# The last steps of the second FFN product in another order, with five instead of four steps that put off P2 and Q4

## The chip, the cores and the metric

The kernel runs on one core of one Trainium2 chip. What counts is the device time of one execution, in microseconds (us). The kernel before takes 1906.04 us (median of 3 runs, 1905.92 to 1906.49).

## The reference, cut to what matters

One layer of a decoder trunk for 520 tokens (512 of a prompt, 8 single ones), in float32. The change touches only the end of it: the second product of the MLP, the residual and the last norm.

```python
x = x + jnp.einsum('blm,md->bld', mix, p['w_out'][l])
hf = rms_norm(x, p['norm_ffn'][l])
ff = jnp.square(jax.nn.relu(jnp.einsum('bld,df->blf', hf, p['w_ff1'][l])))   # 2048 -> 8192
x = x + jnp.einsum('blf,fd->bld', ff, p['w_ff2'][l])                         # 8192 -> 2048
y = rms_norm(x, p['norm_final'])
```

## The kernel before

Features lie on the 128 partitions and the 520 tokens along a row, in two halves of 260 (`c0` and `c1`). The second FFN product has 64 k-tiles of 128 (the 8192 inner features) and 16 output tiles `X[m]`. k-tiles are taken in 32 pairs and outputs in 8 pairs (`ma`, `mb`), and each 2x2 block product is done with seven products instead of eight: P1, P2, P3, Q4, P5, P6, P7 (table `PROD`). Their left sides are the four weight blocks `w11`, `w12`, `w21`, `w22` and four sums of them, `s1` to `s4`; VectorE makes the sums (`sums`, line 1128). Each left side is split into a high part, by ScalarE (`whi`, line 1172), and a low part, by VectorE (`wlo`, line 1174); TensorE then does three matmuls of 260 columns for each pair of k-tiles (lines 1194, 1196, 1197).

A *step* (`Quad` in the code) is one output pair over a stretch of pairs of k-tiles. `ENDS` and `windows()` list the 44 steps of the second product, numbered 0 to 43 here: for every step the output pair `i` and the pairs of k-tiles. The number of pairs in a step is its width; all its operations are 128 columns wide for each pair, so a step of width 7 has weights of 896 columns, and one of width 2 has 256. The last eight steps before are: 36 to 39, output pairs 4 to 7, width 7 each; 40 to 43, output pairs 0 to 3, widths 5, 4, 3 and 2.

The order of work is written out in `items`: for each step P1, then P3 of the step before it, P2, Q4 of the step before it, P6, P7, P5. Steps 40 to 43 are *late*: their P2 and Q4 are left out there and come at the end of the list, behind everything else. P2 and Q4 add only to the columns `c0`, so that after the last other product the columns `c1` of all outputs are done. The main loop goes through `items`, one per iteration; it issues the sums and the split of the item three ahead (`split_item`), then the matmuls of the item (`product`), and what follows from its result (`ff2_done`), some of it put off by one or more iterations (`after`). Each engine runs its own instructions in the order in which they are issued. `whi` and `wlo` have 4 buffers each; the raw weights have 7 (`NRAW`), loaded on SyncE's queue (`more_weights`, line 1098), which waits until a buffer's last reader is done. P2 and Q4 of a late step load `w12` and `w22` a second time.

The last norm needs the sum of squares over all features. A step that ends its output pair (`q.done`) squares the finished tiles (`sq`; ScalarE, line 982). For a step that is not late, VectorE adds the square of the whole tile to one of two tiles `fsum` (line 977). A late step finishes its tiles in four halves, and each half's square goes to TensorE, which adds it over the partitions with a matmul by ones into the tile `side` (`feature_sum`, line 964); this text calls such a matmul a *sum*. At item `H1_DONE`, the first of the products put off, TensorE also sums the two `fsum` tiles, and from two items later `last_norm(1)` runs between the products: square root on ScalarE, a reciprocal and three operations on VectorE (lines 1243 to 1246), then 16 products with the norm (line 1250) three per item, and their stores. When all products are done, `last_norm(0)` does the same for `c0`.

Of the kernel before, what the change touches and what calls it, by code (L numbers as in the profile page):

```python
# [43 lines left out]
class Gap:  # L44


    def __init__(self, n=2):
# [2 lines left out]

ENDS = ((3, 4, 5, 6, 7, 7, 7, 7), (9, 10, 11, 12, 13, 13, 13, 13), (15, 16, 17, 18, 19, 19, 19, 19),
        (21, 22, 23, 24, 25, 25, 25, 25), (27, 28, 29, 30, 32, 32, 32, 32), (32,) * 8)

# [1 line left out]
PAIRS = (30, 0, 1, 2, 31) + tuple(range(3, 30))  # L59


def windows():

    at = [0] * 8
    for ends in ENDS:
        for i, e in enumerate(ends):
            if e > at[i]:
                yield i, at[i], e
                at[i] = e


def trunk_kernel(tc, xT, vecs, w_in, w_out, w_ff1, w2, ca_st, h0_st, cb_st, gate_w, sgu_wT, sgu_b,
# [4 lines left out]
    with ExitStack() as es:  # L77
# [255 lines left out]
        for kh in (0, 1):  # L333
            for j in range(16):
                m = j // 2 + j % 2 * 8 if kh else j
# [16 lines left out]
        quads = []  # L352
# [476 lines left out]
        ffo = [Ops() for _ in range(32)]  # L829
# [136 lines left out]
        def sq(m, sl):  # L966

            n, x = m % 2, X[m][0]
            if fsum[n] is None:
                fsum[n] = cp.tile([128, T], F32, tag=f"ssum{n}", name=nm("fsum"))  # L970
                after(1, lambda: S.activation(out=fsum[n], in_=x, func=AF.Square), "a")
                return
            z = Zt()

            def add():
                if sl is both:
                    V.tensor_tensor(out=fsum[n], in0=fsum[n], in1=z, op=ALU.add)
                else:
                    feature_sum(int(sl is c1), z, m == 7)

            def f():
                S.activation(out=z[:, sl], in_=x[:, sl], func=AF.Square)
                after(1, add, "v" if sl is both else "p")
            after(1, f, "a")
# [68 lines left out]
        off = 0  # L1053
        last_of = {}
        WIN = list(windows())
        for n, (i, a, b) in enumerate(WIN):
            src = w2[off:off + 4 * 128 * 128 * (b - a)].rearrange("(j p c) -> j p c", j=4, p=128)
            quads.append(Quad(src, b - a, [ffo[k] for k in PAIRS[a:b]], i, n, b == 32, n >= 8 * (len(ENDS) - 1)))
            off += 4 * 128 * 128 * (b - a)
            for k in PAIRS[a:b]:  # L1060
                last_of[k] = quads[-1]
# [41 lines left out]
        for q in quads[32:]:  # L1103
            i, a, b = WIN[q.win]
# [77 lines left out]
        def product(k):  # L1182
# [31 lines left out]
            if q.win is None and p == "P1":  # L1214
                if 2 <= q.idx < 18:
                    sum_x1(q.idx - 2)
                elif q.idx == 20:
                    make_S2()
            if q.late and q.idx == 0 and p == "P1":
                add_eps()  # L1220
            (ff1_done if q.win is None else ff2_done)(q, p)

# [215 lines left out]
```

## Time and profile before

| | us |
|---|---|
| median of 3 runs | 1906.04 |
| profiled execution, its own time | 1908.77 |
| its span | 1907.1 |
| TensorE busy (share of the span) | 1885.5 (99%) |
| VectorE busy | 1559.3 (82%) |
| ScalarE busy | 969.3 (51%) |

The profiled execution is a run of its own, so its time stands beside the median and is not one of the three. A matmul of 260 columns has a record of about 0.28 us, but TensorE starts the next one before it ends; the distance from start to start is what a matmul costs. VectorE's records overlap in the same way by somewhat less than 0.1 us. In the timeline the time in square brackets is how long the engine was idle before the instruction, and for what.

### The profile page before, as it was taken

To read this page: it belongs to the slowest core of one execution; us is meant where nothing else is said; L and a number is where in the kernel's file an instruction comes from. 1 tells how busy PE (TensorE), PEld (TensorE's weight loads), DVE (VectorE), ACT (ScalarE), POOL (GpSimd) and SP (SyncE) were. 2 spreads that over 40 slices of the span, in tenths; PEclk is the share of its full clock that TensorE was granted. 3 is DMA by queue.
4 is the path that set the end of the run, shared out by engine and by line. 5 is a ranking of instruction groups with operands and counts; after the bars stand their busy time and mean duration, and the time that the engine had idled before them with its cause. 6 is when DMAs were issued, how large, how long until landed. Compare 5 with 4: busy or idle time off the path is not lost.

```text
span 1907.1 us, 38101 instructions
## 1 busy us (share of the span) xinstructions
PE 1885.5 (99%) x15588; PEld 1879.3 (99%) x15588; DVE 1559.3 (82%) x2186; ACT 969.3 (51%) x1443; POOL 248.4 (13%) x471
## 2 busy tenths in 40 slices
PE   9999999999999999999999999999999999999996
PEld 9999999999999999999999999999999999999996
DVE  7878777575688889889888888877798888888887
ACT  7345445562235666666665666644444444444453
POOL 0000000000000222122112111500312212112000
PEclk9999999999999999999999999999999999999998
DMA  7323223132343666656656556853756657647334
GB/s 253 106 95 115 73 96 114 59 139 104 126 167 124 217 205 211 217 199 218 209 178 212 196 193 207 288 188 102 277 165 235 231 190 237 207 152 259 119 90 135
DMA packets 110832, 329.36 MB, mean 173 GB/s; under 512 B 16320, under 2 KB 25152, under 8 KB 110656
## 3 DMA queue, kind: packets, MB, share of 16 engines
q1 hardware_dynamic: 73200, 205.35, 32.6%
q0 software_dynamic: 36160, 120.37, 17.8%
q8 instruction: 122, 2.00, 0.4%
q10 hardware_dynamic: 1296, 1.19, 0.2%
q14 instruction: 54, 0.44, 0.1%
HBM read 261.71 MB, written 65.15 MB: 171 GB/s over the span
## 4 chain that ended last, share of the span: by engine, by line
PE 96%; DVE 2%; DMA 1%; issue 0%; ACT 0%; SPq 0%; DVEq 0%
PE psA L1197 12%; PE psA L1194 12%; PE psA L1196 12%; PE ps L192 10%; PE ps L190 10%; PE ps L188 10%; PE psD L1194 6%; PE psD L1196 6%; PE psD L1197 6%; PE psB L1197 3%; PE psB L1196 3%; PE psB L1194 3%; DMA raw<-w 1%; DVE X L1250 1%; DVE wlo L1174 0%
## 5 line engine op out<-in xcount | busy, mean ns | idle before, releaser
L1172 ACT ACTIVATE whi<-raw 128x1024 fp32r<-128x1024 f32 (+5 forms) x532 | 489.2, 922 | 327.6 <-PE psD L1196 149.2
L1174 DVE TENSOR_TENSOR wlo<-raw,whi 128x1024 fp32r<-128x1024 f32 (+5 forms) x532 | 559.8, 1053 | 89.6 <-ACT whi L1172 88.1
L1197 PE MATMUL psA<-o,wlo 128*128 128x260 f32 x2048 | 579.3, 283 | 2.1 <-DVE wlo L1174 2.1
L1194 PE MATMUL psA<-o,whi 128*128 128x260 f32 x2048 | 579.1, 283 | 1.0 <-ACT z L1213 0.5
L1196 PE MATMUL psA<-o,whi 128*128 128x260 f32 x2048 | 578.1, 282 | 0.0
L1197 PEld LDWEIGHTS psA<-o,wlo 128*128 128x128 f32 x2048 | 385.6, 188 | 2.5 <-DVE wlo L1174 2.5
L1194 PEld LDWEIGHTS psA<-o,whi 128*128 128x128 f32 x2048 | 385.7, 188 | 1.7 <-ACT z L1213 0.7
L1196 PEld LDWEIGHTS psA<-o,whi 128*128 128x128 f32 x2048 | 385.6, 188 | 0.1
L1128 DVE TENSOR_TENSOR raw<-raw,raw 128x1024 f32<-128x1024 f32 (+6 forms) x304 | 319.3, 1050 | 28.0 <-DMA raw<-w 27.6
L188 PE MATMUL ps<-Ah,whi 128*128 128x260 f32 x1536 | 311.5, 284 | 1.2 <-ACT Ah L367 1.2
L190 PE MATMUL ps<-Al,whi 128*128 128x260 f32 x1536 | 310.8, 284 | 0.0
L192 PE MATMUL ps<-Ah,wlo 128*128 128x260 f32 x1536 | 310.4, 283 | 0.0
L1194 PE MATMUL psD<-o,whi 128*128 128x260 f32 x1024 | 291.1, 284 | 0.0
L1196 PE MATMUL psD<-o,whi 128*128 128x260 f32 x1024 | 289.8, 283 | 0.0
L1197 PE MATMUL psD<-o,wlo 128*128 128x260 f32 x1024 | 288.8, 282 | 0.0
L188 PEld LDWEIGHTS ps<-Ah,whi 128*128 128x128 f32 x1536 | 238.5, 189 | 2.0 <-ACT Ah L367 1.8
L192 PEld LDWEIGHTS ps<-Ah,wlo 128*128 128x128 f32 x1536 | 238.3, 189 | 0.0
L190 PEld LDWEIGHTS ps<-Al,whi 128*128 128x128 f32 x1536 | 237.5, 190 | 0.6 <-DVE Al L370 0.6
L920 POOL DMA_DIRECT2D fx<-o x210 | 114.0, 543 | 819.6 <-DVE o L805 561.8
L1196 PEld LDWEIGHTS psD<-o,whi 128*128 128x128 f32 x1024 | 193.0, 188 | 0.2
L1194 PEld LDWEIGHTS psD<-o,whi 128*128 128x128 f32 x1024 | 192.7, 188 | 0.2
L1197 PEld LDWEIGHTS psD<-o,wlo 128*128 128x128 f32 x1024 | 192.8, 188 | 0.0
(212 smaller groups left out, 2291.5 us busy)
## 6 DMA issues: line engine op xcount, KB each, us to landing
raw<-w_ff SPq DMA_DIRECT2D x128, 512.0 KB, 4.1
fx<-o POOLq DMA_DIRECT2D x210, 260.0 KB, 2.9
o<-fx POOLq DMA_DIRECT2D x210, 260.0 KB, 5.1
raw<-w SPq DMA_DIRECT2D x116, 384.0 KB, 3.8
raw<-w_in SPq DMA_DIRECT2D x62, 512.0 KB, 6.1
raw<-w_out SPq DMA_DIRECT2D x32, 512.0 KB, 5.6
raw<-w SPq DMA_DIRECT2D x32, 448.0 KB, 3.4
z<-x1d POOLq DMA_DIRECT2D x32, 260.0 KB, 3.1
```

The source lines that it names most:

```text
L188: PE.matmul(ps[:, h, :H], hi[:, kk], xh[:, h * H:(h + 1) * H], start=st, stop=False)
L190: PE.matmul(ps[:, h, :H], hi[:, kk], xl[:, h * H:(h + 1) * H], start=False, stop=False)
L192: PE.matmul(ps[:, h, :H], lo[:, kk], xh[:, h * H:(h + 1) * H], start=False, stop=sp)
L920: P.dma_start(fxd[i][2 * g - 1 + n if g else 0], t[0][:, :].bitcast(F32))
L1128: V.tensor_tensor(out=o[0][:, :n], in0=x[0][:, :n], in1=y[0][:, :n], op=ALU.add)
L1172: S.activation(out=whis[i][:, :n], in_=r[0][:, :n], func=AF.Copy)
L1174: V.tensor_tensor(out=wlos[i][:, :n], in0=r[0][:, :n], in1=whis[i][:, :n].bitcast(F32), op=ALU.subtract)
L1194: PE.matmul(ps, hi[:, kk], xh, start=first and j == 0, stop=False, skip_group_check=True)
L1196: PE.matmul(ps, hi[:, kk], xl, start=False, stop=False, skip_group_check=True)
L1197: PE.matmul(ps, lo[:, kk], xh, start=False, stop=j == q.q - 1 and p in (("P2", "P3", "Q4", "P7") if q.late else ("P2", "P3", "Q4")), skip_ ...
L1250: V.scalar_tensor_tensor(out=x, in0=x, scalar=vc(V_FIN + m), in1=o, op0=ALU.mult, op1=ALU.mult)
```

## The change

`ENDS` loses its last row and its steps of width 7 for output pairs 4 to 7; the steps that finish the outputs are now listed by `LAST`, in the order of the output pairs 4, 0, 1, 5, 2, 6, 3, 7. The last eight steps, 36 to 43, thus have the widths 7, 5, 4, 7, 3, 7, 2, 7. The last five of them, 39 to 43 (output pairs 5, 2, 6, 3, 7), are late, where before it was the last four. Steps 0 to 35 are as before. `add_eps` moves with the first late step. The weights in memory (`w2`) follow the order of the steps. Two loads more are issued, since one step more loads `w12` and `w22` twice.

```diff
--- before.py
+++ after.py
@@ -50,8 +50,10 @@
 
 
 
+
+LAST = (4, 0, 1, 5, 2, 6, 3, 7)
 ENDS = ((3, 4, 5, 6, 7, 7, 7, 7), (9, 10, 11, 12, 13, 13, 13, 13), (15, 16, 17, 18, 19, 19, 19, 19),
-        (21, 22, 23, 24, 25, 25, 25, 25), (27, 28, 29, 30, 32, 32, 32, 32), (32,) * 8)
+        (21, 22, 23, 24, 25, 25, 25, 25), (27, 28, 29, 30, 25, 25, 25, 25))
 
 
 
@@ -67,6 +69,8 @@
             if e > at[i]:
                 yield i, at[i], e
                 at[i] = e
+    for i in LAST:
+        yield i, at[i], 32
 
 
 def trunk_kernel(tc, xT, vecs, w_in, w_out, w_ff1, w2, ca_st, h0_st, cb_st, gate_w, sgu_wT, sgu_b,
@@ -976,7 +980,7 @@
                 if sl is both:
                     V.tensor_tensor(out=fsum[n], in0=fsum[n], in1=z, op=ALU.add)
                 else:
-                    feature_sum(int(sl is c1), z, m == 7)
+                    feature_sum(int(sl is c1), z, m == 15)
 
             def f():
                 S.activation(out=z[:, sl], in_=x[:, sl], func=AF.Square)
@@ -1053,9 +1057,10 @@
         off = 0
         last_of = {}
         WIN = list(windows())
+        LATE = len(WIN) - 5
         for n, (i, a, b) in enumerate(WIN):
             src = w2[off:off + 4 * 128 * 128 * (b - a)].rearrange("(j p c) -> j p c", j=4, p=128)
-            quads.append(Quad(src, b - a, [ffo[k] for k in PAIRS[a:b]], i, n, b == 32, n >= 8 * (len(ENDS) - 1)))
+            quads.append(Quad(src, b - a, [ffo[k] for k in PAIRS[a:b]], i, n, b == 32, n >= LATE))
             off += 4 * 128 * 128 * (b - a)
             for k in PAIRS[a:b]:
                 last_of[k] = quads[-1]
@@ -1216,7 +1221,7 @@
                     sum_x1(q.idx - 2)
                 elif q.idx == 20:
                     make_S2()
-            if q.late and q.idx == 0 and p == "P1":
+            if q.win == LATE and p == "P1":
                 add_eps()
             (ff1_done if q.win is None else ff2_done)(q, p)
```

VectorE, from the addition that follows step 41's P3 (the tiles `X`) to the low part of step 43's P6 (step 43 is the last one). Before, where step 42 has width 3 and step 43 width 2:

```order
L998 TENSOR_TENSOR X_15410<-X_15410,psA_23092 128x260
L1128 TENSOR_TENSOR raw_23236<-raw_23130,raw_23196 128x256
L1174 TENSOR_TENSOR wlo_23239<-raw_23130,whi_23238 128x256
L1128 TENSOR_TENSOR raw_23196<-raw_23196,raw_23215 128x256
L1128 TENSOR_TENSOR raw_23130<-raw_23196,raw_23130 128x256
L1174 TENSOR_TENSOR wlo_23258<-raw_23061,whi_23257 128x384
L1032 TENSOR_TENSOR X_15560<-X_15560,psD_23262 128x520
L1128 TENSOR_TENSOR raw_23176<-raw_23130,raw_23176 128x256
L1174 TENSOR_TENSOR wlo_23279<-raw_23130,whi_23278 128x256
```

The same place after the change, where step 42 has width 2 and step 43 width 7:

```order
L1002 TENSOR_TENSOR X_16302<-X_16302,psA_22911 128x260
L1133 TENSOR_TENSOR raw_23090<-raw_22952,raw_23044 128x896
L1179 TENSOR_TENSOR wlo_23093<-raw_22952,whi_23092 128x896
L1133 TENSOR_TENSOR raw_23044<-raw_23044,raw_23060 128x896
L1133 TENSOR_TENSOR raw_22952<-raw_23044,raw_22952 128x896
L1179 TENSOR_TENSOR wlo_23109<-raw_22886,whi_23108 128x256
L1036 TENSOR_TENSOR X_15730<-X_15730,psD_23113 128x520
L1133 TENSOR_TENSOR raw_23015<-raw_22952,raw_23015 128x896
L1179 TENSOR_TENSOR wlo_23127<-raw_22952,whi_23126 128x896
```

The kinds of rows and their order are the same: an addition, the sum `s3` and the low part of step 43's P1, the sums `s1` and `s2`, the low part of step 42's P3, an addition to `X` over both halves, the sum `s4` and the low part of step 43's P6. Those of step 43 are 896 instead of 256 columns wide, and that of step 42 is 256 instead of 384.

VectorE in the part where the products put off run and `last_norm(1)` goes on between them (the low parts are those of the P2 and Q4 put off, `RF` is the norm of the columns c1). Before:

```order
L1174 TENSOR_TENSOR wlo_23469<-raw_23357,whi_23468 128x256
L1002 TENSOR_TENSOR X_15411<-X_15411,psD_23474 128x260
L1250 SCALAR_TENSOR_TENSOR X_15307<-X_15307,vec,RF 128x260
L1250 SCALAR_TENSOR_TENSOR X_15308<-X_15308,vec,RF 128x260
L1250 SCALAR_TENSOR_TENSOR X_15410<-X_15410,vec,RF 128x260
L1174 TENSOR_TENSOR wlo_23496<-raw_23370,whi_23495 128x256
L998 TENSOR_TENSOR X_15559<-X_15559,psB_23501 128x260
L1250 SCALAR_TENSOR_TENSOR X_15411<-X_15411,vec,RF 128x260
L1250 SCALAR_TENSOR_TENSOR X_15559<-X_15559,vec,RF 128x260
L1250 SCALAR_TENSOR_TENSOR X_15560<-X_15560,vec,RF 128x260
L1002 TENSOR_TENSOR X_15560<-X_15560,psD_23521 128x260
```

After the change, at the same point behind the three operations that end in `RF`:

```order
L1179 TENSOR_TENSOR wlo_23423<-raw_23272,whi_23422 128x256
L1002 TENSOR_TENSOR X_16302<-X_16302,psB_23428 128x260
L1255 SCALAR_TENSOR_TENSOR X_15411<-X_15411,vec,RF 128x260
L1255 SCALAR_TENSOR_TENSOR X_15559<-X_15559,vec,RF 128x260
L1255 SCALAR_TENSOR_TENSOR X_15560<-X_15560,vec,RF 128x260
L1179 TENSOR_TENSOR wlo_23459<-raw_23303,whi_23458 128x896
L1006 TENSOR_TENSOR X_16303<-X_16303,psD_23464 128x260
L1255 SCALAR_TENSOR_TENSOR X_15729<-X_15729,vec,RF 128x260
L1255 SCALAR_TENSOR_TENSOR X_15730<-X_15730,vec,RF 128x260
L1255 SCALAR_TENSOR_TENSOR X_15906<-X_15906,vec,RF 128x260
L1179 TENSOR_TENSOR wlo_23495<-raw_23340,whi_23494 128x896
L1002 TENSOR_TENSOR X_15729<-X_15729,psB_23500 128x260
```

Before, the last two low parts (of step 43's P2 and Q4) are 256 wide and are the first and the sixth row behind `RF`; after them come additions and products with the norm alone. Now the low parts of step 43's P2 and Q4 are 896 wide and stand further on, between the products with the norm, each ahead of an addition to `X` that a square and a sum on TensorE follow.

## Rows read from the trace of the kernel before

**Rows 1.** The page, part 1: busy time, share of span, instructions.
```profile
PE 1885.5 (99%) x15588; PEld 1879.3 (99%) x15588; DVE 1559.3 (82%) x2186; ACT 969.3 (51%) x1443; POOL 248.4 (13%) x471
```

**Rows 2.** Busy time by stretch: us, PE, PEld, DVE, ACT, POOL, granted clock, DMA, GB/s.
```profile
1780.00:1842.00 62.00, 62.00 (x520) 62.00 (x519) 51.48 (x66) 29.38 (x40) 0.00 (x0) 1.00 0.32 93
1249.60:1253.20 3.60, 2.97 (x13) 2.67 (x13) 1.63 (x3) 0.00 (x0) 0.00 (x0) 0.54 0.36 118
1884.00:1891.70 7.70, 6.11 (x38) 5.05 (x36) 7.60 (x21) 1.98 (x5) 0.00 (x0) 1.00 0.38 131
```

**Rows 3.** Waits of TensorE: who for whom, total us, times, longest.
```profile
PE side L964 <- ACT z L982: 2.2, 2, 1.4
```

**Rows 4.** Timeline 1881 to 1883: start us, us, engine, line, operation [idle before].
```profile
1881.82 0.28 PE L1197 MATMUL psB<-o,wlo 128*128 128x260 f32 x1
...
1881.93 0.60 PE L964 MATMUL side<-z,ones 128*128 128x260 f32 x2
...
1882.14 0.43 DVE L998 TENSOR_TENSOR X<-X,psB 128x260 f32<-128x260 f32 x1 [0.83 <-PE psB L1197]
...
1882.48 1.77 DVE L1243 RECIPROCAL RF<-z 128x260 f32<-128x260 f32 x1
1882.49 0.28 PE L1196 MATMUL psD<-o,whi 128*128 128x260 f32 x1
```

**Rows 5.** Timeline 1885 to 1888, the same columns.
```profile
1885.20 0.28 PE L1197 MATMUL psB<-o,wlo 128*128 128x260 f32 x1
...
1885.56 0.42 DVE L1174 TENSOR_TENSOR wlo<-raw,whi 128x256 fp32r<-128x256 f32 x1
1885.89 0.42 DVE L1002 TENSOR_TENSOR X<-X,psD 128x260 f32<-128x260 f32 x1
...
1886.41 0.42 ACT L982 ACTIVATE z<-X 128x260 f32<-128x260 f32 x1 [2.10 <-DVE X L1002]
...
1886.88 0.71 PE L964 MATMUL side<-z,ones 128*128 128x260 f32 x2 [1.40 <-ACT z L982]
...
1887.54 0.28 PE L1196 MATMUL psD<-o,whi 128*128 128x260 f32 x1
...
1887.77 0.42 DVE L998 TENSOR_TENSOR X<-X,psB 128x260 f32<-128x260 f32 x1
...
1888.10 1.28 DVE L1250 SCALAR_TENSOR_TENSOR X<-X,vec,RF 128x260 f32<-128x260 f32 x3
...
1889.30 0.42 DVE L1002 TENSOR_TENSOR X<-X,psD 128x260 f32<-128x260 f32 x1
```

**Rows 6.** Timeline, the end of the last product.
```profile
1891.37 0.28 PE L1197 MATMUL psD<-o,wlo 128*128 128x260 f32 x1
...
1892.37 0.42 DVE L1002 TENSOR_TENSOR X<-X,psD 128x260 f32<-128x260 f32 x1
```

**Rows 7.** Timeline of TensorE around step 43's P5 and P3.
```profile
1872.26 0.28 PE L1197 MATMUL psA<-o,wlo 128*128 128x260 f32 x1
1873.02 0.39 PE L1194 MATMUL psA<-o,whi 128*128 128x260 f32 x1 [0.48 <-ACT z L1213]
```

**Rows 8.** Timeline of VectorE and, last, ScalarE: wide operations.
```profile
1823.54 1.08 DVE L1128 TENSOR_TENSOR raw<-raw,raw 128x896 f32<-128x896 f32 x1
1824.54 1.09 DVE L1174 TENSOR_TENSOR wlo<-raw,whi 128x896 fp32r<-128x896 f32 x1
1825.54 0.42 DVE L998 TENSOR_TENSOR X<-X,psA 128x260 f32<-128x260 f32 x1
...
1837.50 0.95 ACT L1172 ACTIVATE whi<-raw 128x896 fp32r<-128x896 f32 x1 [1.23 <-issue]
```

**Rows 9.** DMA issues by line, 1780 to 1880: KB each, median us to landing.
```profile
raw<-w SPq DMA_DIRECT2D x8, 448.0 KB, 3.3
```

**Rows 10.** Tile view of raw, 1780 to 1890: its loads.
```profile
DMA to landing us min/median/max: 2.0/2.9/4.2
```

**Rows 11.** Timeline of TensorE behind its longest pause in the second product.
```profile
1249.59 0.58 PE L1197 MATMUL psA<-o,wlo 128*128 128x260 f32 x1 [1.91 <-DVE wlo L1174]
```

## What the change does to the time, predicted

> **What bounds the kernel now.** I read the page's busy shares first: TensorE is busy for 99% of the span, VectorE for 82%, ScalarE for 51% [rows 1]. A busy share says little of TensorE, because its records overlap, so the next view is the table of stretches: 520 matmuls in the 62 us before the narrow steps, one every 0.119 us, at full granted clock [rows 2]. In wide steps nothing stands between two matmuls. Then come TensorE's waits and the timeline of the last 50 us. There TensorE pauses in two places. Between the last P5 and P3, which share a PSUM tile, it waits for ScalarE's copy: 0.76 us from start to start instead of 0.12 [rows 7]. Among the products put off it waits for squares [rows 3]. That chain is worth following back: the sum at 1886.88 waited for a square at 1886.41, that for an addition on VectorE at 1885.89, and the addition stood in VectorE's order behind the reciprocal of 1882.48, three operations and a low part [rows 4, 5]. So at the end VectorE sets the pace, and TensorE everywhere else. When the last matmul is issued, at 1891.37, its addition starts 1.00 us later, since VectorE is still at the norm of c1; in a case without a queue, 1881.82 to 1882.14, it is 0.32 [rows 4, 6]. What follows that addition is a chain of fixed work for c0 which the change leaves alone.
>
> **What the change does not touch.** Steps 0 to 36 give the same instructions in the same order. The last eight steps have 42 pairs of k-tiles in both orders, so 42 x 7 x 3 = 882 matmuls in both, at 0.119 us each the same 105 us. (A product of width w takes 3 w x 0.119: 2.5 us at 7, 1.07 at 3, 0.72 at 2.) What can differ is what stands between the matmuls.
>
> **Added: four sums on TensorE.** One step more is late, and each late step has four sums of squares by TensorE: 20 instead of 16. (Two full-width `fsum` additions leave VectorE for it, in a place where nobody waits.) A sum costs TensorE 0.67 - 2 x 0.12 = 0.43 us between 1881.82 and 1882.49 [rows 4], and 0.66 - 0.12 = 0.54 us between 1886.88 and 1887.54 [rows 5]. I take 0.5: +2.0 us. All four lie in TensorE's path: two in step 40, where step 39's halves are summed, two behind the first products put off.
>
> **Removed: the pauses at the end before.** From 1885.20 to 1886.88 TensorE loses 1.68 - 0.12 = 1.56 us. From there to 1891.49 (0.12 after the last start) there are 21 matmuls and three sums, 21 x 0.119 + 3 x 0.54 = 4.1 of 4.6 us: 0.5 more [rows 5, 6]. Together -2.06. The last addition no longer queues: 1.00 - 0.32 = -0.68.
>
> **What takes the place of these pauses.** The closing chain keeps its place, two products behind `H1_DONE`, and the products around it are now 40's (width 3), 41's (7), 42's (2) and 43's (7). I count from the moment at which TensorE has issued step 40's P2. VectorE: addition at 0.2, reciprocal at 0.54, low part 3.08 later (1882.48 to 1885.56), the addition for 40's Q4 at 3.95. From an addition's start to its sum is 0.99 us (1885.89 to 1886.88) [rows 4, 5]. That sum can run at 4.94. TensorE arrives there after sum, Q4, sum and 41's P2, 0.5 + 1.07 + 0.5 + 2.5 = 4.57: a pause of 0.4. Then VectorE has three products with the norm (1.20, 1888.10 to 1889.30), a narrow low part (0.33), an addition (0.33), three products, and then a low part of 896 columns, which takes 1.00 (1824.54 to 1825.54) [rows 5, 8]: 41's Q4 is added at 8.36, summed at 9.35; TensorE arrives at 9.16: 0.2. Three more products with the norm and the second wide low part put the addition for 42's P2 at 10.9 and its sum at 11.9, where TensorE arrives at 10.6: 1.3. Behind that VectorE gets ahead, and the two last wide products run free. Together +1.9: step 42 is too short to cover VectorE's work, and that work has grown by the wide low parts. So of the 2.06 us removed nearly all comes back in another place.
>
> **Bursts ahead of a wide step.** Before, a step is at most as wide as the one before it from step 36 on. Now a wide step follows a narrow one three times. Its two sums `s1`, `s2`, the sums `s3` and `s4` and the low parts of P1 and P6 are due on VectorE while TensorE runs the narrow products. For step 43, counted from the end of 41's P3: VectorE's addition at 0.2, then s3, low part, s1, s2 at 1.00 each, 42's low part 0.33, an addition over 520 columns (0.6, between 0.33 for 260 and 1.00 for 896), s4, and the low part of 43's P6 until 7.6. TensorE: two sums, three narrow products of 0.72, P1 2.5, 42's P3 0.72, and 0.24 to the first matmul that takes a low part: 6.6. One wait inside lies on the way: the second sum's square stands on ScalarE behind a wide high part of 0.95 [rows 8] and is 0.4 late. So 1.0 us is lost. For step 41 the same count gives VectorE 7.7 and TensorE 8.0, since step 40's products are 1.07: nothing. For step 39, behind step 38 of width 4, both come out at about 10, if `w21` lands 3.3 us after its issue [rows 9]: 0.2. Together +1.2. The rows before show no step that widens here, so this term has only bounds: 0 (the counts are off by under 1 us each, and TensorE, already at one matmul every 0.119 us, can gain nothing below it), and 3.9, if each of the three is 0.9 later, by the longest landing of 4.2 instead of 3.3 [rows 10]. I keep 1.2, nearest to the rows.
>
> The Trainium skill (VectorE: DVE Perf Modes, The DRAIN you can't avoid) says that "the next op does not start until the 8-stage pipe empties", though it adds that an operation which is not held starts earlier. The rows show starts 1.00 apart for records of 1.08 and 1.09 [rows 8], so by the trace the pipe is not emptied first. By the page's first sentence the burst of step 43 and the two wide low parts at the end would take about 0.7 us more, and the sum below would be +3.0.
>
> **No change elsewhere.** The wait between the last P5 and P3 stays: the copy does not depend on the width [rows 7]. The loads of the products put off, now 448 KB for the wide ones, are issued at least four wide products (4 x 2.5 = 10 us) ahead of their split, against 3.3 to landing [rows 9].
>
> **Sum.** +2.0 - 2.06 + 1.9 + 1.2 - 0.68 = +2.4 us on the profiled execution: span 1907.1 to 1909.5, its own time 1908.77 to 1911.2. That execution stands 2.7 us above the median of the runs; the same +2.4 on the median is 1908.4.
>
> **Rivals.** A measurement of this kernel can tell about 0.2%, 3.8 us, from no change.
>
> *The pauses do go away.* The products put off last longer (52 pairs instead of 28), and if ScalarE and VectorE get to the squares 1 us sooner than I count, only the four sums remain against what is saved: 2.0 - 2.06 - 0.68 + 0.2 = -0.5, 1905.5. Further down, if bursts and sums fill only time that was lost anyway, it is -2.7, 1903.3. For it: VectorE is idle for stretches in wide steps. Against: its order is fixed, and the wide low parts stand ahead of the additions.
> The Trainium skill (Perfetto Trace Analysis, Optimization Strategy) says that where the most-contended engine changes over time, interleaving those regimes may help; here that would be this rival, since narrow steps are VectorE's and wide ones TensorE's. The trace bears out the two regimes, but also that TensorE lost nothing in the narrow steps before.
>
> *Slower: VectorE late for every wide step.* All three bursts start 0.9 late, because a raw buffer comes free only when the narrow step lets go of it and the load lands at 4.2 instead of 3.3 [rows 9, 10]: +2.7. A pause then reaches the 1.91 after which, at 1249.59, the granted clock had a mean of 0.54 over 3.6 us, most of it at the lower level of 1.2 GHz [rows 11, 2]; around the pause of 1.40 at 1886 it stayed at 1.00 [rows 5, 2]. 3.6 x (1 - 0.54) = 1.7 us of work are lost by that. Then 2.4 + 2.7 + 1.7 = +6.8, 1912.8. It decides from pauses of 1.9 us on. Against: the loads of this stretch are small, and no wait of VectorE for one is seen after 1780.
>
> *The change does nothing visible:* the terms cancel; this is the forecast read with 0.2% as a bound.
>
> **Chances.** The forecast, 1907 to 1909.8: 0.50. The pauses gone, or less lost than I count, 1903 to 1907: 0.30, of which 0.04 is faster by over 0.2%. Slower, from 1909.8 up: 0.20. So faster 0.04, same 0.76, slower 0.20. The range is 1904.6 to 1911.0: it takes in the bursts at nothing and the bursts near their upper bound without the clock.
>
> **What would show it.** Right: 40 instead of 32 matmul records for the sums of squares on `side`; TensorE's waits name `side` after ScalarE's square with about 1.9 us among the products put off, the longest just before 43's P2, and `psA` or the low part of step 43's P6 with about 0.6. The last addition starts 0.3 us after the last matmul. Wrong: no wait on `side` at all (then 1905.5), a wait of VectorE for `raw` from DMA, or a stretch after 1780 with a granted clock under 1.

## The result, and the profile after

The changed kernel takes 1918.03 us (median of 6 runs, 1915.11 to 1922.57), the kernel before in the same session 1906.26 (1905.31 to 1910.66, 6 runs): a ratio of 1.0058, interval 1.0048 to 1.0068. That is +11.8 us where +2.4 was forecast, outside the range. The profiled execution of the changed kernel took 1915.11, the least of its runs. In the new code the lines stand four or five further down: the sums of squares are L968 (964 before), the square is L986 (982), VectorE's additions and subtractions to `X` are L1002 and L1006 (998 and 1002), the sums of weights L1133 (1128), the splits L1177 and L1179, the matmuls L1199, L1201 and L1202.

The page of the changed kernel, busy time and count of each engine (answers to [rows 1]), and two of its groups:

```profile
PE 1886.2 (99%) x15596; PEld 1878.2 (98%) x15596; DVE 1555.7 (81%) x2184; ACT 968.1 (51%) x1445; POOL 249.1 (13%) x471
...
L1179 DVE TENSOR_TENSOR wlo<-raw,whi 128x1024 fp32r<-128x1024 f32 (+6 forms) x532 | 559.0, 1051 | 85.4 <-ACT whi L1177 84.8
L1199 PE MATMUL psA<-o,whi 128*128 128x260 f32 x2048 | 578.9, 283 | 2.9 <-DVE X L1002 1.9
```

Busy shares say nothing of it: they are those of before. TensorE's waits from the copy behind step 36's P6 (`z<-psA`, 1780.09) to its last matmul do. The row for `side` answers to [rows 3], of which 1.4 us lie in the same stretch before, and the row for `psA` after `z` to [rows 7]; the middle row is new:

```profile
PE side L968 <- ACT z L986: 4.4, 4, 1.7
PE psA L1199 <- DVE X L1002: 1.9, 3, 1.6
PE psA L1199 <- ACT z L1218: 0.5, 1, 0.5
```

Columns: engine, what it writes and what it waits for; us in total, times, longest. Together 6.8 us, against 1.4 + 0.5 = 1.9 before. The stretch from that copy to the last matmul is 117.91 us (1780.09 to 1898.00); before it is 109.13 (1782.24 to 1891.37). So 8.8 us arise here, 4.9 of them as waits in these rows.

The three places where a wide step follows a narrow one, timelines of TensorE (start, duration, instruction, and in brackets the wait ahead). Step 39:

```profile
1817.10 0.36 PE L1199 MATMUL psA<-o,whi 128*128 128x260 f32 x1 [1.57 <-DVE X L1002]
```

Step 41, all engines:

```profile
1836.10 0.69 DVE L1006 TENSOR_TENSOR X<-X,z 128x520 f32<-128x520 f32 x1
1836.71 1.08 DVE L1179 TENSOR_TENSOR wlo<-raw,whi 128x896 fp32r<-128x896 f32 x1
1836.82 0.42 ACT L986 ACTIVATE z<-X 128x260 f32<-128x260 f32 x1 [0.69 <-DVE X L1006]
...
1837.29 0.71 PE L968 MATMUL side<-z,ones 128*128 128x260 f32 x2 [1.05 <-ACT z L986]
1837.71 0.41 DVE L1002 TENSOR_TENSOR X<-X,psA 128x260 f32<-128x260 f32 x1
...
1838.18 0.39 PE L1199 MATMUL psA<-o,whi 128*128 128x260 f32 x1 [0.18 <-DVE X L1002]
1838.40 0.28 PE L1201 MATMUL psA<-o,whi 128*128 128x260 f32 x1
```

And step 43, TensorE:

```profile
1858.36 0.70 PE L968 MATMUL side<-z,ones 128*128 128x260 f32 x2 [1.68 <-ACT z L986]
1859.25 0.39 PE L1199 MATMUL psA<-o,whi 128*128 128x260 f32 x1 [0.18 <-DVE X L1002]
1859.47 0.28 PE L1201 MATMUL psA<-o,whi 128*128 128x260 f32 x1
```

The 0.18 in brackets is not all that this second wait costs. From the start of the sum to the second matmul behind it are 1.11 us in both steps; less 0.12 for a matmul and 0.54 for the sum, the price the prediction found in the same way, 0.45 are left.

What VectorE does ahead of that, its timeline of step 43:

```profile
1849.75 0.43 DVE L1002 TENSOR_TENSOR X<-X,psA 128x260 f32<-128x260 f32 x1 [1.13 <-PE psA L1202]
1850.09 1.08 DVE L1133 TENSOR_TENSOR raw<-raw,raw 128x896 f32<-128x896 f32 x1
1851.09 1.08 DVE L1179 TENSOR_TENSOR wlo<-raw,whi 128x896 fp32r<-128x896 f32 x1
1852.09 2.21 DVE L1133 TENSOR_TENSOR raw<-raw,raw 128x896 f32<-128x896 f32 x2
1854.22 0.42 DVE L1179 TENSOR_TENSOR wlo<-raw,whi 128x256 fp32r<-128x256 f32 x1
1854.56 0.69 DVE L1036 TENSOR_TENSOR X<-X,psD 128x520 f32<-128x520 f32 x1
1855.16 1.08 DVE L1133 TENSOR_TENSOR raw<-raw,raw 128x896 f32<-128x896 f32 x1
1856.16 1.08 DVE L1179 TENSOR_TENSOR wlo<-raw,whi 128x896 fp32r<-128x896 f32 x1
1857.17 0.69 DVE L1006 TENSOR_TENSOR X<-X,z 128x520 f32<-128x520 f32 x1
1857.78 1.08 DVE L1179 TENSOR_TENSOR wlo<-raw,whi 128x896 fp32r<-128x896 f32 x1
1858.78 0.41 DVE L1002 TENSOR_TENSOR X<-X,psA 128x260 f32<-128x260 f32 x1
```

VectorE has no gap from 1849.75 to 1859.12. The low part of 43's P6 (1856.16) is where the prediction stopped counting. But TensorE needs two more results ahead of P6's first matmul. The first is the sum of squares of step 42's last half: its square follows the subtraction at 1857.17, which stands behind that low part. The second is P1's PSUM tile, in which P6 goes on: VectorE first adds P1 from it to `X`, at 1858.78, behind the low part of P7. The three places show these two waits: step 39 the second alone (step 38 is not late and has no sum on TensorE), steps 41 and 43 both.

In step 39 a load comes on top. VectorE's timeline there:

```profile
1805.58 0.42 DVE L1006 TENSOR_TENSOR X<-X,psD 128x260 f32<-128x260 f32 x1
1807.63 1.09 DVE L1133 TENSOR_TENSOR raw<-raw,raw 128x896 f32<-128x896 f32 x1 [1.62 <-DMA raw<-w]
```

That load of `w21` was issued at 1803.16 and landed about 4.4 us later. From 1807.63 to the addition of P1 at 1816.54 VectorE has no gap, so whatever the load is late goes on to TensorE's wait at 1817.10.

The end came in total about as forecast: TensorE's pauses among the products put off (answers to [rows 5]), and the last matmul with VectorE's addition to it (to [rows 6]).

```profile
1885.39 0.49 PE L968 MATMUL side<-z,ones 128*128 128x260 f32 x1 [0.80 <-ACT z L986]
...
1892.12 0.49 PE L968 MATMUL side<-z,ones 128*128 128x260 f32 x1 [0.86 <-ACT z L986]
...
1898.00 0.28 PE L1202 MATMUL psD<-o,wlo 128*128 128x260 f32 x1
...
1898.32 0.42 DVE L1006 TENSOR_TENSOR X<-X,psD 128x260 f32<-128x260 f32 x1 [2.12 <-PE psD L1202]
```

### The profile page after: what moved, and what is told of

Same layout as the page of the kernel before. It is cut to its first block, busy times and chain, and to the rows that moved or that the text cites. A ratio compares the mean times of both kernels' runs of the same rounds, so it can differ in the third digit from the quotient of the medians.

```text
span 1913.4 us, 38121 instructions
## 1 busy us (share of the span) xinstructions
PE 1886.2 (99%) x15596; PEld 1878.2 (98%) x15596; DVE 1555.7 (81%) x2184; ACT 968.1 (51%) x1445; POOL 249.1 (13%) x471
## 4 chain that ended last, share of the span: by engine, by line
PE 96%; DVE 2%; DMA 1%; issue 1%; ACT 0%; SPq 0%; DVEq 0%; ACTq 0%
PE psA L1199 12%; PE psA L1202 12%; PE psA L1201 12%; PE ps L196 10%; PE ps L194 10%; PE ps L192 10%; PE psD L1199 6%; PE psD L1201 6%; PE psD L1202 6%; PE psB L1202 3%; PE psB L1199 3%; PE psB L1201 3%; DVE wlo L1179 1%; DMA raw<-w 1%; DVE X L1255 1%
## 5 line engine op out<-in xcount | busy, mean ns | idle before, releaser
L1177 ACT ACTIVATE whi<-raw 128x1024 fp32r<-128x1024 f32 (+6 forms) x532 | 488.0, 921 | 329.1 <-PE psD L1201 142.9
L1179 DVE TENSOR_TENSOR wlo<-raw,whi 128x1024 fp32r<-128x1024 f32 (+6 forms) x532 | 559.0, 1051 | 85.4 <-ACT whi L1177 84.8
L1199 PE MATMUL psA<-o,whi 128*128 128x260 f32 x2048 | 578.9, 283 | 2.9 <-DVE X L1002 1.9
L1202 PE MATMUL psA<-o,wlo 128*128 128x260 f32 x2048 | 578.8, 283 | 1.9 <-DVE wlo L1179 1.9
L1201 PE MATMUL psA<-o,whi 128*128 128x260 f32 x2048 | 577.7, 282 | 0.0
L1199 PEld LDWEIGHTS psA<-o,whi 128*128 128x128 f32 x2048 | 385.3, 188 | 5.0 <-ACT z L993 1.7
L1202 PEld LDWEIGHTS psA<-o,wlo 128*128 128x128 f32 x2048 | 385.1, 188 | 2.3 <-DVE wlo L1179 2.2
L1201 PEld LDWEIGHTS psA<-o,whi 128*128 128x128 f32 x2048 | 385.2, 188 | 0.1
L1133 DVE TENSOR_TENSOR raw<-raw,raw 128x1024 f32<-128x1024 f32 (+4 forms) x304 | 318.9, 1049 | 37.0 <-DMA raw<-w 36.6
L1199 PE MATMUL psD<-o,whi 128*128 128x260 f32 x1024 | 291.5, 285 | 0.0
L1201 PE MATMUL psD<-o,whi 128*128 128x260 f32 x1024 | 289.8, 283 | 0.0
L1202 PE MATMUL psD<-o,wlo 128*128 128x260 f32 x1024 | 289.0, 282 | 0.0
L1201 PEld LDWEIGHTS psD<-o,whi 128*128 128x128 f32 x1024 | 193.0, 188 | 0.3
L1202 PEld LDWEIGHTS psD<-o,wlo 128*128 128x128 f32 x1024 | 192.8, 188 | 0.2 <-DVE wlo L1179 0.2
L1199 PEld LDWEIGHTS psD<-o,whi 128*128 128x128 f32 x1024 | 192.7, 188 | 0.3
```

Of the source, the lines that this page charges most:

```text
L1133: V.tensor_tensor(out=o[0][:, :n], in0=x[0][:, :n], in1=y[0][:, :n], op=ALU.add)
L1177: S.activation(out=whis[i][:, :n], in_=r[0][:, :n], func=AF.Copy)
L1179: V.tensor_tensor(out=wlos[i][:, :n], in0=r[0][:, :n], in1=whis[i][:, :n].bitcast(F32), op=ALU.subtract)
L1199: PE.matmul(ps, hi[:, kk], xh, start=first and j == 0, stop=False, skip_group_check=True)
L1201: PE.matmul(ps, hi[:, kk], xl, start=False, stop=False, skip_group_check=True)
L1202: PE.matmul(ps, lo[:, kk], xh, start=False, stop=j == q.q - 1 and p in (("P2", "P3", "Q4", "P7") if q.late else ("P2", "P3", "Q4")), skip_ ...
```

## The experiments

*Tail* means the time from the copy behind step 36's P6 to the end of the span: 124.9 us in the profile before, 133.3 in that of the changed kernel. Unlike the span it leaves out the part that both have in common, in which the two profiled executions happen to differ by 2.15 us. A *pause* is counted from start to start, less 0.12; it is about 0.16 more than the wait in brackets (behind a sum it is counted as the 0.45 above). Each experiment was timed beside the kernel before on its chip.

**1. The changed kernel again.** No edit.

> The changed kernel, unchanged, to see how its executions differ from each other. Both theories see the same place: before P6 of steps 39, 41 and 43 TensorE pauses for some 2 us each. If the granted clock is what spreads the times (1915 to 1923), then this profile either shows all three pauses below 1.9 us, the clock at 1.00 after 1800 and a time near 1915, or a longer pause with a clock near 0.5 for some 3.6 us behind it and a time about 2 us longer for each. If the spread comes from the earlier part of the kernel, the stretch after 1785 is as long as in the first profile (128 us) whatever the time.

1917.76 us (1916.23 to 1918.74), ratio 1.0049 [1.0036, 1.0063]. The waits are the same ones. The tail is 134.7, though, 1.4 more than in the first profile. The stretch behind the wait of 1.68 in step 43 shows why: first the changed kernel's first profile, then this one.

```profile
1860.00:1864.00 4.00, 4.00 (x34) 3.94 (x34) 2.21 (x4) 1.65 (x3) 0.00 (x0) 1.00 0.78 249
```

```profile
1860.00:1864.00 4.00, 3.89 (x20) 3.89 (x21) 2.39 (x4) 0.43 (x2) 0.00 (x0) 0.57 0.71 207
```

Columns: stretch, its length, busy time and count of TensorE's matmuls and weight loads, VectorE, ScalarE, GpSimd, then the granted clock, DMA share and GB/s. Behind the same pause the clock is at 1.00 in one execution and largely at the lower level of 1.2 GHz in another: 20 instead of 34 matmuls in 4 us. That costs 1.4 us of tail, where about 2 were expected, and the pause was not a longer one, as the expectation had it.

**2. The order of before, five steps late.** Only one half of the change.

```diff
-LAST = (4, 0, 1, 5, 2, 6, 3, 7)
+LAST = (4, 5, 6, 7, 0, 1, 2, 3)
...
-                    feature_sum(int(sl is c1), z, m == 15)
+                    feature_sum(int(sl is c1), z, m == 7)
```

> Half of the change: the widths keep the old order (7, 7, 7, 7, 5, 4, 3, 2 in steps 36 to 43), but step 39 is late as well, so that five steps put off P2 and Q4. Theory (the wide step behind a narrow one costs the time): no step widens, so no wait for the addition of P1; four sums more (+2.0), and longer products put off around the closing chain (-0.5 to -1.5): 1906.5 to 1908.5. Rival (putting off five steps costs the time, by the sums, the second loads and the closing chain): most of the +11.8, so 1913 or more.

1909.12 (1907.29 to 1911.57), ratio 1.0007 [0.9998, 1.0016]; tail +1.4. From 1780 to 1840 TensorE's matmuls are busy without a gap; pauses stand only among the products put off, 1.27 and 0.33. So one late step more can't be told from no change in the time, though the median is 0.6 above the expected range: its four sums, about 2.0 us, are paid for in part by the shorter pauses at the end (1.6 instead of 2.06).

**3. The change's order, four steps late.** The other half.

```diff
-        LATE = len(WIN) - 5
+        LATE = len(WIN) - 4
```

> The other half: the widths alternate as in the change (7, 5, 4, 7, 3, 7, 2, 7), but only the last four steps, 40 to 43, are late, as before. Step 39 then has P2 and Q4 between P1 and P6. Theory: the pauses before P6 of steps 41 and 43 stay at about 2 us each, that of step 39 goes; with the same 16 sums: +3.5 to +7 on before (the upper end if the clock falls behind a pause), 1910 to 1913. Rival (five late steps are the cost): within 1 us of before.

1916.43 (1913.63 to 1918.51), ratio 1.0042 [1.003, 1.0055], more than the expected 1910 to 1913. The order alone costs most of it. The pauses stand at 1839.83 (1.62), 1842.64 (1.62) and 1864.93 (1.84), and the clock falls three times in this profile, the third time among the products put off, behind waits of 1.33 and 1.12 (tail 135.5):

```profile
1840.00:1850.00 10.00, 8.54 (x53) 7.75 (x54) 7.33 (x12) 3.83 (x7) 0.00 (x0) 0.83 0.37 118
1860.00:1870.00 10.00, 8.07 (x49) 7.25 (x48) 8.11 (x11) 4.59 (x7) 0.00 (x0) 0.84 0.55 164
1890.00:1900.00 10.00, 7.55 (x46) 6.83 (x44) 7.61 (x18) 2.09 (x5) 0.00 (x0) 0.83 0.36 121
```

**4. P1 added before the next split.** In late steps the addition of P1, which frees P6's PSUM tile, is issued ahead of the low part of P7.

```diff
+            early = i >= NP and items[i - NP][1] == "P1" and items[i - NP][0].late
+            if early:
+                run_due("p", i)
+                product(i - NP)
             if NP <= i + AHEAD < NU:
                 split_item(i + AHEAD - NP)
...
-                product(i - NP)
+                if not early:
+                    run_due("p", i)
+                    product(i - NP)
```

> The changed kernel, with the addition of a late step's P1 to its output issued ahead of the sums and the split of the item three ahead, instead of behind them. Theory: P6 goes on in the PSUM tile of P1, so it waits for that addition, and the addition stands behind a wide low part; now it doesn't. The wait for DVE X before P6 goes (0.65 us in steps 41 and 43, more in 39); the wait for the sum of squares before it stays, since that square still stands behind the burst: 1 to 3 us faster than the change, more if the clock no longer falls: 1911 to 1916. Rival (P6 waits for its own low part, as the prediction had it): no difference.

1912.97 (1911.55 to 1916.97), ratio 1.0031 [1.0021, 1.004]. By the medians that is 4.8 us less than the changed kernel on the same chip, by the ratios 3.4, with intervals that overlap. TensorE's waits from 1780 to 1900 have no row for `psA <- DVE X` any more:

```profile
PE side L968 <- ACT z L986: 5.1, 5, 1.7
PE psA L1202 <- DVE wlo L1179: 1.2, 1, 1.2
PE psA L1199 <- ACT z L1218: 0.5, 1, 0.5
```

So the addition behind the wide low part was one of the two waits. The sum of squares stays, with pauses of 1.40 and 1.83, and step 39 now waits 1.2 for the next thing in VectorE's order, a low part. The trace shows much less than the clocked times: the tail is 133.8 us. The clock falls behind the wait of 1.67 in step 43,

```profile
1840.00:1860.00 20.00, 18.14 (x131) 17.23 (x130) 15.77 (x24) 9.35 (x18) 0.00 (x0) 0.93 0.46 147
```

so the tail to compare with is the 134.7 of experiment 1, which has such a fall too: 0.9 less. Where the rest of the clocked gain lies no trace here shows.

**5. P7 moved ahead of P6 in late steps,** to put 2.5 us of TensorE's work in front of the pause.

```diff
+            if q1 is not None and q1.late:
+                seq = [(q1, "P1"), (q1, "P7"), (q1, "P6"), (q0, "P3"), (q0, "Q4"), (q1, "P5")]
```

> The changed kernel with another order of products inside the five late steps: P1, P7, P6, then P3 of the step before, then P5, instead of P1, P3 of the step before, P6, P7, P5. P7 has a PSUM tile of its own, so 2.5 us of a wide step now lie between P1 and P6, where the change has a product of 0.7 to 1.4 us. Theory (TensorE has too little work between P1 and P6 while VectorE works off the burst and the addition of P1): the three pauses ahead of P6 (1.9, 1.9 and 2.6 us in the first profile of the change) shrink to under 1 us each, and the clock falls less often: 5 to 9 us faster than the change, 1909 to 1913. Rival (VectorE as a whole is the limit in this stretch, so that a pause only moves): no more than 2 us faster than the change, with the pauses in another place.

1919.4 (1918.38 to 1920.4), ratio 1.0071 [1.0059, 1.0084]: a miss. The pauses moved and grew; those of steps 41 and 43:

```profile
1836.00 1.05 PE L968 MATMUL side<-z,ones 128*128 128x260 f32 x2 [2.06 <-ACT z L986]
...
1859.49 0.49 PE L968 MATMUL side<-z,ones 128*128 128x260 f32 x1 [2.65 <-ACT z L986]
```

Behind both the granted clock falls (0.57 from 1836 to 1840 and from 1860 to 1864), which is part of the loss. Another order of products does not shorten VectorE's burst; it only decides which of its results is waited for, and P7 early wants its low part early as well.

**6. The kernel before, with the products put off in the order of widths 3, 2, 4, 5.**

```diff
-        items += [(q, p) for q in quads if q.late for p in ("P2", "Q4")]
+        PUT_OFF = [quads[-2], quads[-1], quads[-3], quads[-4]]
+        items += [(q, p) for q in PUT_OFF for p in ("P2", "Q4")]
...
```

The loads of these products follow the same order.

> The kernel before, its widths and four late steps unchanged, but the products put off run in the order of steps 42, 43, 41, 40 (widths 3, 2, 4, 5) instead of 40 to 43 (5, 4, 3, 2). Two short products instead of two long ones stand ahead of the closing chain, and the longer ones run beside it. Theory (TensorE pauses where a product put off is shorter than VectorE's work beside it): the pauses for sums of squares at the end, 2.1 us, and the last addition's wait of 0.7 shrink by 1 to 2 us together: 0.5 to 2 us faster than before, little for the clocked times, plain in the trace. Rival (the closing chain on VectorE is the whole of the end, whatever TensorE does beside it): same length, within 0.5 us.

1907.26 (1905.69 to 1911.05), ratio 1.001 [1.0001, 1.0019]; tail -0.2. The pauses become 2.15 and 0.29 in place of 1.56 and 0.5. That is the rival's case: in this order too the closing chain on VectorE decides how long the end is, and TensorE's pauses only move.

**7. One change of width instead of three:** the steps of width 5, 4, 3, 2 first, then four wide ones, four late.

```diff
-LAST = (4, 0, 1, 5, 2, 6, 3, 7)
+LAST = (0, 1, 2, 3, 4, 5, 6, 7)
...
-        LATE = len(WIN) - 5
+        LATE = len(WIN) - 4
```

> The outputs finish in the order 0 to 7: steps 36 to 43 have the widths 5, 4, 3, 2, 7, 7, 7, 7, and the last four, all wide, are late. Only step 40 is wide behind a narrow one (width 2). Theory: one pause of 2 to 3 us ahead of step 40's P6, none ahead of the P6 of steps 41 to 43, where the P3 between is wide; no pauses among the products put off, which are all wide; and 2 to 5 us lost in the narrow steps, which now do seven products and the full-width squares on VectorE: 1908 to 1913. Rival (a wide late step is slow by itself): a pause ahead of P6 in each of the four late steps, 1914 or more.

1911.33 (1911.02 to 1913.14), ratio 1.0032 [1.002, 1.0044], 8.1 us less than experiment 5 on the same chip, and by the ratios 3 to 5 less than the changed kernel. No pause stands ahead of P6 in steps 42 and 43, nor among the products put off. What is left lies around the one place where the width grows, from 2 in step 39 to 7 in step 40:

```profile
1806.47 0.39 PE L1199 MATMUL psA<-o,whi 128*128 128x260 f32 x1 [1.63 <-ACT z L1216]
1809.76 0.39 PE L1202 MATMUL psA<-o,wlo 128*128 128x260 f32 x1 [2.06 <-DVE wlo L1179]
1816.55 0.36 PE L1199 MATMUL psA<-o,whi 128*128 128x260 f32 x1 [1.28 <-DVE X L1002]
1829.92 0.71 PE L968 MATMUL side<-z,ones 128*128 128x260 f32 x2 [0.56 <-ACT z L986]
```

These are pauses of 1.80 ahead of step 39's P5, 2.23 in step 40's P1, 1.44 ahead of step 40's P6, and 0.71 and 0.45 still ahead of step 41's P6, where none was expected: 6.6 us, no less than the three places of the changed kernel cost together, and the clock falls behind them (0.84 and 0.73 from 1808 to 1816). By these rows the gain on the changed kernel lies elsewhere: four sums fewer, and no pauses among the products put off.

**8. TensorE kept busy in the pauses:** five matmuls of 128 columns into a tile that nobody reads, ahead of P6 in steps 39, 41 and 43.

```diff
+                if items[i - NP][1] == "P6" and items[i - NP][0].win in (39, 41, 43):
+                    fill = ps2[0].tile([128, H], F32, tag="B", name=nm("fill"), bufs=2)
+                    for _ in range(5):
+                        PE.matmul(fill[:, :128], ones, ones, start=True, stop=True, skip_group_check=True)
```

> The changed kernel with five small matmuls (128 columns of ones, into a PSUM tile that nobody reads) in TensorE's order just ahead of the sum of squares and of P6 in steps 39, 41 and 43. They are about 1 us of work in pauses of 1.7 to 2.6 us, which VectorE sets, so the pauses end no later, but TensorE idles for under 1.5 us at a time. Theory of the clock (part of the slowdown is the clock that falls behind these pauses in some executions): no granted clock under 1 from 1800 to 1880, tail as long as in the first profile of the change (133.3 us from the copy of step 36's P6), and clocked times 2 to 4 us below those of the change. Rival (the clock has no share): times within 1 us of the change.

1914.54 (1913.45 to 1916.69), ratio 1.0045 [1.0033, 1.0058]. The tail is 133.1 and the granted clock 1.00 all the way from 1800 to 1900. Experiment 10, without the filling and on the same chip, took 1.5 us more, with a fall of the clock. The two intervals overlap, so the times alone don't show a share of the clock; the tails, 133.1 and 134.7, put it at about 1.5 us in an execution with a fall, less than the 2 to 4 expected.

**9. Part of VectorE's work on GpSimd:** in late steps the sum `s3` and the subtraction of P5.

```diff
-                    sub(mb, both, q.raw["u"])
+                    if q.late:
+                        o = X[mb][0]
+                        P.tensor_tensor(out=o, in0=o, in1=q.raw["u"], op=ALU.subtract)
+                    else:
+                        sub(mb, both, q.raw["u"])
...
+                e = P if q.late and w == "s3" else V
```

> The changed kernel with two of VectorE's operations of the late steps on GpSimd, which is idle here: the sum s3 (1.0 us for the wide steps) and the subtraction over both halves that follows P5 (0.6 us). Theory (VectorE's burst in its order sets the pauses ahead of P6): VectorE gets to P6's low part and to the addition of P1 1.0 to 1.6 us earlier in steps 41 and 43, so those pauses shrink by about that: 2 to 5 us faster than the change. Rival (the pauses come from TensorE's own order of products and sums): within 1 us of the change, or slower if GpSimd's operations come late.

1917.49 (1917.39 to 1919.14), ratio 1.0062 [1.0049, 1.0074]: a miss. The tail is 136.8, with a fall of the clock (0.87 and 0.70 from 1836 to 1844); that is 2.1 us longer than the changed kernel's with a fall. VectorE is slowed beside GpSimd; one place, the sum and the low part for step 41's P1:

```profile
1827.64 2.11 POOL L1138 TENSOR_TENSOR raw<-raw,raw 128x896 f32<-128x896 f32 x1 [2.01 <-DMA raw<-w]
...
1828.16 2.53 DVE L1184 TENSOR_TENSOR wlo<-raw,whi 128x896 fp32r<-128x896 f32 x1 [0.49 <-ACT whi L1182]
```

The low part takes 2.53 instead of 1.08. It ends at 1830.69, and GpSimd's record at 1829.75: it looks as if VectorE did its work only behind GpSimd's, which is read from these two records and not tested by itself. The Trainium skill (SBUF — State Buffer, SBUF: two separate sides) says that VectorE with two inputs in SBUF and GpSimd share one pair of ports, which whoever comes first holds for its whole instruction. These two records agree with it.

**10. The changed kernel a third time,** beside 8 and 9. No edit.

> The changed kernel once more, on the same chip as the two kernels before it in this list, to compare them with. Expected 1915 to 1920; each execution with a granted clock under 1 behind a pause of about 1.7 us should be 1.5 to 2 us longer in its tail.

1916.07 (1915.83 to 1918.61), ratio 1.0056 [1.0041, 1.0072]; tail 134.7, with the clock at 0.57 from 1858 to 1862, behind the same wait of 1.68. That is 1.4 us longer than the first profile, where 1.5 to 2 was expected.

**11. The kernel before, with every fourth product of the last norm on GpSimd.**

```diff
+            for m in range(1, 16, 4):
+                S.activation(out=X[m][0][:, sl], in_=X[m][0][:, sl], func=AF.Copy, scale=vc(V_FIN + m))
...
+                if m % 4 == 1:
+                    P.tensor_tensor(out=x, in0=x, in1=o, op=ALU.mult)
...
-                (S if m % 2 and not h else nc.sync).dma_start(yT[m][:, sl], x)
+                (S if m % 2 == 0 and not h else nc.sync).dma_start(yT[m][:, sl], x)
```

The stores of `c0` change queues with it: ScalarE's takes the even tiles instead of the odd ones.

> The kernel before with every fourth product with the final norm taken from VectorE: ScalarE scales the tile by the norm's weight ahead of time, GpSimd multiplies it by the norm. Theory (VectorE is the limit of the last 25 us, beside which TensorE waits): TensorE's pauses among the products put off shrink by 0.5 to 1 us, and the last run of products on VectorE (6.5 us) by 1.6: 1.5 to 3 us faster than before. Rival (the stores or GpSimd's products end last): no gain.

1907.99 (1906.36 to 1910.95), ratio 1.0009 [1.0, 1.0017]: no gain. Its 24 products left on VectorE take 598 ns each in the mean, the 32 of the kernel before 484: what is taken from VectorE it loses beside GpSimd. The last run of products, 16 in 6.49 us before, is 12 in 6.79 us.

**12. The sums `s1` and `s2` of steps 39, 41 and 43 cut to 128 of 896 columns.** The rest of these sums is left out of what is computed; TensorE does the same as in the changed kernel.

```diff
-            n = q.q * 128
+            n = 128 if q.win in (39, 41, 43) and w in ("s1", "s2") else q.q * 128
```

> The order is the change's. In steps 39, 41 and 43 the two sums s1 and s2 add only the first 128 of their 896 columns, so their result leaves out the rest; TensorE's work is the same. Theory (the pauses are VectorE's burst ahead of a wide step, counted to the square and to the addition of P1): two records of 2.21 us together become about 0.4, so VectorE is about 1.8 us earlier at each of these places. The pauses of 1.73 in step 39 and 1.21 + 0.65 in step 41 go, and of 1.83 + 0.65 in step 43 about 0.6 is left. The stretch from the copy behind step 36's P6 to the end, 133.3 us with the change where the clock stays up, becomes 128 (127.3 to 129), no granted clock under 0.95 behind these places, and the time is 6 to 9 us under the change's, about 1909 (ratio to before 1.001 to 1.003). Rival 1 (the limit is not VectorE's length but when buffers and loads come, or ScalarE's squares): the pauses stay within 0.5 us of what they are and the time is 1914 or more. Rival 2 (as when P7 was moved: the pauses move to the next place): VectorE's wait for raw weights or TensorE's wait for a low part takes 1 us or more in each of the three steps, the stretch is 131 or more.

1908.8 (1907.66 to 1911.02), ratio 1.0016 [1.0006, 1.0026]; tail 128.7, where 128 was expected. The pause of step 39 is gone, step 41's is 0.37, and in step 43 this is left, 0.72 and 0.28:

```profile
1853.08 0.71 PE L968 MATMUL side<-z,ones 128*128 128x260 f32 x2 [0.56 <-ACT z L986]
1853.79 0.39 PE L1199 MATMUL psA<-o,whi 128*128 128x260 f32 x1
```

The clock stays at 1.00 up to 1880. Only about 1.6 us of VectorE's time in each of three steps was taken away (the two sums take 0.61 instead of 2.21), and 4.7 us of tail went; by the ratios it is 6 to 8 us, in which falls of the clock can have a part. VectorE's wait for `w21` in step 39 is still there (1.5); behind shorter sums it costs TensorE nothing.

## Why the prediction was wrong

**The step that failed: bursts ahead of a wide step.** The prediction gave them +1.2 (1.0 in step 43, 0.2 in step 39, none in step 41), with 3.9 as the upper bound. They measure 1.73 in step 39, 1.21 + 0.45 in step 41 and 1.83 + 0.45 in step 43, 5.7 us in all, and two pauses of 0.3 beside them: 6.3. The durations that went into the count were right; VectorE's rows of step 43 can be laid beside it one by one. Its end was wrong: it stopped at the low part of P6, as if TensorE ran on until it needs that. Its two sums on TensorE are those of step 41; the one of step 42, ahead of P6, is not in it. In TensorE's own order the narrow step's sum of squares and the use of P1's PSUM tile come before, and both hang on VectorE instructions that stand behind that low part: the subtraction that follows P5, the low part of P7, the addition of P1. That is 1.6 us of VectorE's time in step 43, from 1857.17 to 1858.78, and as much in 41. Experiment 12 shortens the burst itself and leaves 1.4 us of these pauses; that shows the burst as their cause. Experiment 4 takes away the wait for P1's tile, which is worth 0.9 us of tail at a like clock. Step 39 is a case of its own: `w21` was counted at 3.3 us to landing and took 4.4. As VectorE has no gap behind it, a landing at 3.3 would have left about 0.9 of the 2.0 lost there (1.73 and one of the pauses of 0.3); that is an estimate from the rows of this step, and no run takes the late load away. It is the place at which the slower rival's mechanism came about, once instead of three times: no wait of VectorE for a load stands in steps 41 and 43.

**The upper bound failed with it.** It allowed each burst 0.9 more for a late load, and nothing for a wrong end of the count.

**The clock.** The slower rival let it fall from pauses of 1.9 on. It fell behind waits of 1.68 (experiments 1 and 10), and not behind the same wait in the first profile. The first profile, without a fall, has the tail at +8.45, experiments 1 and 10 have it at +9.8. How far the fall explains the spread of the other runs, up to 1922.57, is not shown: they have no trace. The Trainium skill (TensorE: Matmul & The Clock Gate, What's actually happening) says that the chip's window of observation runs freely, so that the same kernel changes its clock at different places from run to run; it says so of the rise at a kernel's start. A fall in two of three executions fits that, but no run here shows the window.

**What was right.** Four more sums (40 instead of 32 records for `z` on `side`). The pauses among the products put off: 0.96, 0.25 and 1.02, 2.2 in all, where 1.9 was forecast as 0.4, 0.2 and 1.3; that the sum comes so near is in part luck, since the first is 0.6 longer and the last 0.3 shorter than counted. The wait between the last P5 and P3, 0.48. The last addition 0.32 behind the last matmul; of the 0.68 saved there only 0.33 arrive at the end of the span (15.40 us from the last matmul instead of 15.73), since the chain behind it is a little longer.

**The account.** +2.0 (sums) - 2.06 (pauses of before) + 2.2 (products put off) + 5.7 + 0.6 (bursts) - 0.33 (end) = +8.1 of the 8.45 by which the tail is longer without a fall of the clock. The 0.3 left over are gaps under 0.3 us that were not placed one by one. With a fall it is +9.8, and the medians of the three sets of runs are 9.3 to 11.8 above before.

**The rivals.** That the pauses go away was wrong by the most. The slower rival, at +6.8, came nearest in time, but for a reason that held in one step of three. Experiments 2 and 3 show that it was the order of widths and not the fifth late step: 1.0007 for the one, 1.0042 for the other. None of the versions tried beats the kernel before.

## What to carry to other kernels

When work of two widths alternates, count the burst of the in-order helper engine up to the last result that the main engine needs ahead of its next instruction, in the main engine's own order: accumulators that must be read out first and small reductions in between count as much as operands. An average of 81% busy on the helper says nothing there; it is the stretch in which the wide step's preparation meets the narrow step's short cover. An order in which the widths only fall had no such pauses (the kernel before, experiment 2). To gather the growth in one place does not help by itself: in experiment 7 one growth from 2 to 7 cost 6.6 us around it.

## What the runs showed of the hardware

A wait of 1.68 us on a TensorE that was busy before and after brought the granted clock down in two profiles of the changed kernel and not in the third, at 1.4 us of tail each time. And GpSimd was no help here for a VectorE that is short of time: a `TENSOR_TENSOR` over 896 columns took GpSimd 2.11 us, and VectorE's own beside it took 2.53 instead of 1.08.
